# Low parts of 32 weight tiles made on GpSimd, with their loads and stores in its queue

## The chip, the cores and the metric

One core of a Trainium2 chip runs the kernel. The metric is the device time of one execution in microseconds (us); the median of three runs is compared. Engine names are those of the profile: PE is TensorE's matmul, PEld its weight load, ACT ScalarE, DVE VectorE, POOL GpSimd and SP SyncE; a q behind a name is the engine's instruction queue where it issues a DMA or waits.

## What is computed

One layer of a decoder block on a sequence of 1024 tokens with 1024 channels, in float32. The branch points are these:

```python
h = rms_norm(x, norm_gain) * (1.0 + scale) + shift      # scale, shift, gate from silu(c) @ w_ada + b_ada
q, k, v, z_a, u, z_b, m_a, m_b = split(h @ w_in)        # eight parts of 1024 columns
p_a = (stick_breaking_attention(q, k, v) * silu(z_a)) @ w_branch_a    # 16 heads of 64
p_b = (multiscale_causal_pool(u, pool_w, pool_scale) * silu(z_b)) @ w_branch_b
merged = sigmoid(m_a) * p_a + sigmoid(m_b) * p_b
out = rms_norm(x + gate * (merged @ w_out), final_gain)
```

## The kernel before

Every large product is made of three matmuls on TensorE. Each operand is split in two float32r parts: a high part, which is a copy of the operand, and a low part, the operand minus its high part. High by high, high by low and low by high are summed in PSUM. The weights come from HBM as float32 tiles of 128 x 1024, so each has to be split on the chip.

The stages follow one another on PE. First h is normed, turned and split, while the u projection of the first half of the tokens is begun. Then come the second half of u (to 128.7 us), the v projection (128.9 to 218 us), the eight z_b projections (tiles `wzb`, to 317.5 us), seven products of the pooling branch (names p1 to p7, to 395 us), then attention with the remaining 40 column tiles of w_in (k, q, z_a, m_a, m_b) projected between its steps (to 1032 us), and the end: w_branch_a, the merge, w_out and the last norm.

The 40 late column tiles are listed in `tiles`, in the order in which attention asks for them. For the first eight (`PLAIN`), `load_parts` splits the weight when it is needed, with the copy on ACT and the subtraction on POOL (or on DVE for one). For the other 32 the low part is made much earlier and put into an HBM tensor, `wl_d`; `load_parts` then reads the weight and the low part and only copies the high part again. Making it early is the work of `make_lo`, called once after each u tile (eight tiles), in the v loop by `LO_V` (ten), in the z_b loop by `LO_ZB` (four) and after the products by `LO_PB` (ten). A call takes a buffer tagged `lraw`, loads the weight into it, copies it to `lhi` (which has one buffer), subtracts `lhi` from `lraw` in place and stores the result. Within the v loop the last three steps are put off by one turn of the loop (`later=True`).

In the u and v stages these buffers lie in the pool `vp`, which is closed when v is done; its memory then goes to the pool `pb` of the z_b stage and the products. In `pb` the tag `lraw`, with three buffers, is also used by `gjunk` and by the gate weights `wg`: row j of w_gate is loaded, multiplied by silu(c), held in `sg`, and summed by DVE to one column of `gate`.

In the z_b stage PE writes halves of 24 matmuls into two PSUM banks in turn (tag `pj`). `silu` empties a bank: a sigmoid on ACT (L663) and a product on DVE (L664) that reads the bank; after L664 the bank is free. In the v stage L609 on ACT and L610 on DVE do the same.

The order of the instructions of each engine is drawn up ahead of time by a scheduler, which ranks them by their place in the program and by its own simulated times; where `order` or `keep_in_program_order` is used the program's order is kept, as in the first stage and in attention. The engines then run their queues strictly in that order. An instruction that has to wait, for a tile or for a buffer, holds everything behind it in its queue. Before the change SP's queue issues the loads and the stores of `make_lo`.

Of the kernel before, what the change touches and what calls it, by code (L numbers as in the profile page):

```python
# [9 lines left out]
F32 = mybir.dt.float32  # L10
F32R = mybir.dt.float32r
# [4 lines left out]
P = 128  # L16
D = 1024
# [23 lines left out]
LO_ZB = (0, 1, 0, 1, 0, 1, 0, 1)  # L41
LO_PB = (1, 2, 1, 2, 1, 2, 1)
# [15 lines left out]
def block_kernel(ctx, tc, a, out):  # L58
    nc = tc.nc
    v, act, gp = nc.vector, nc.scalar, nc.gpsimd  # L60

    def pool(name, **kw):
        return tc.tile_pool(name=name, bufs=1, reuse_waits="tile", **kw)
# [9 lines left out]
    def bank(tag, name):  # L73
        return psp.tile([P, 512], F32, tag=tag, bufs=BANKS[tag], name=name)
# [8 lines left out]
    wl_d = dram.tile([5 * KB, P, D], F32, name="wl_d")  # L83
# [37 lines left out]
    def copy_to(eng, dst, src):  # L121
        if eng is act:
            act.copy(dst, src)
        elif eng is gp:
            gp.tensor_scalar(dst, src, 1.0, 0.0, op0=ALU.mult, op1=ALU.add)
        else:
            v.tensor_copy(dst, src)
# [7 lines left out]
    tiles = []  # L135
# [6 lines left out]
    def make_lo(pl, n, bufs=3, later=False):  # L142

        rest = []
        for _ in range(n):
            i = next(early_lo)
            raw = pl.tile([P, D], F32, tag="lraw", bufs=bufs, name=f"l{i}_raw")
            hi = pl.tile([P, D], F32R, tag="lhi", bufs=1, name=f"l{i}_hi")
            nc.sync.dma_start(raw, a["w_in"][tiles[i]])

            def low(i=i, raw=raw, hi=hi):
                act.copy(hi, raw)  # L152
                v.tensor_sub(raw.bitcast(F32R), raw, hi.bitcast(F32))  # L153
                nc.sync.dma_start(wl_d[i], raw)

            if later:
                rest.append(low)
            else:
                low()
        return rest  # L160
# [27 lines left out]
    def project(ct, name, use, he, le):  # L188
        whl = load_w(a["w_in"][ct], name, he, le)
        for sh in range(2):  # L190
            ps = bank("pj", f"{name}_{sh}")
            mm3(ps, whl, (h_hi, h_lo), range(KB), hmov(sh))
            use(sh, ps)
# [18 lines left out]
    with pool("init") as init:  # L212
# [101 lines left out]
        wg, maps, halves = {}, {}, {}  # L314
# [66 lines left out]
        hi, lo_ = (0,), (1,)  # L381
# [172 lines left out]
    def load_u(j):  # L554
        u = dif.tile([P, S + 16], F32, tag="u", bufs=2, name=f"u{j}")
        v.memset(u[:, S:], 0.0)
        nc.sync.dma_start(u[:, :S], u_d[j])
        return u

    def make_d(j, u):  # L560
        win = WINDOWS[j // 2]
        cur, n, step = u, S + 16, 1
        while step < win:
            nxt = dif.tile([P, S + 16], F32, tag="win", bufs=2, name=f"win{j}_{step}")
            n -= step
            v.tensor_add(nxt[:, :n], cur[:, :n], cur[:, step:step + n])
            cur, step = nxt, 2 * step
        t0 = S - win + 1
        d = dif.tile([P, S], F32, tag="d", bufs=5, name=f"d{j}")
        v.scalar_tensor_tensor(d[:, :t0], cur[:, :t0], 1.0 / win, u[:, :t0], ALU.mult, ALU.subtract)  # L570
        tl = dif.tile([P, 16], F32, tag="tl", bufs=2, name=f"tl{j}")
        v.tensor_mul(tl[:, :win - 1], cur[:, t0:S], invn[:, 16 - win + 1:])
        v.tensor_sub(d[:, t0:], tl[:, :win - 1], u[:, t0:S])
        dhls[j] = d


    with pool("vp") as vp:
# [6 lines left out]
        for i in reversed(range(KB)):  # L584
            ps = bank("pj", f"u{i}_1")
            mm3(ps, whl[i], h, range(KB), hmov(1))
            use[i](1, ps)
            make_lo(vp, 1)
# [6 lines left out]
        for hf in range(2):  # L595
            if hf == 0:
                wv.append([load_wv(1, k2) for k2 in range(4)])
            for sb in range(8):
# [18 lines left out]
                if 8 * hf + sb in DIFFS:  # L617
                    j = DIFFS[8 * hf + sb]
# [8 lines left out]
    pb = pbs.enter_context(pool("pb"))  # L627
# [11 lines left out]
    def b_op(src, name):  # L639
        hl = pb.tile([P, 2, 2, 512], F32R, tag="bhl", bufs=3, name=name)  # L640
        act.copy(hl[:, 0], src)
        v.tensor_sub(hl[:, 1], src, hl[:, 0].bitcast(F32))
        return hl
# [7 lines left out]
    def a_op(src, name):  # L651
        hl = wts.tile([P, 2, 2, 512], F32R, tag="whl", bufs=2, name=name)
        act.copy(hl[:, 0], src)
        v.tensor_sub(hl[:, 1], src, hl[:, 0].bitcast(F32))
        return hl

    for j in range(KB):
        if j not in dhls:
            make_d(j, load_u(j))

        def silu(sh, ps):
            z = gb[:, j, sh * 512:sh * 512 + 512]
            act.activation(z, ps, AF.Sigmoid)  # L663
            v.tensor_mul(z, ps, z)  # L664
            v.scalar_tensor_tensor(z, dhls[j][:, sh * 512:sh * 512 + 512], psc_v[:, j:j + 1], z, ALU.mult, ALU.mult)

        project(CZB + j, f"wzb{j}", silu, act, v)
        if j < 4:
            v.tensor_sub(t1[:, j], gb[:, j, 512:], gb[:, j, :512])
        else:  # L670
            v.tensor_sub(t2[:, j - 4], gb[:, j, 512:], t1[:, j - 4])
            v.tensor_sub(gb[:, j - 4, 512:], gb[:, j, 512:], gb[:, j - 4, 512:])
        make_lo(pb, LO_ZB[j])
        if j == 0:
            nc.sync.dma_start(sg, a["c_row"].broadcast_to([P, D]))
            gjunk = pb.tile([P, D], F32, tag="lraw", bufs=3, name="gjunk")
            act.activation(gjunk, sg, AF.Sigmoid)
            v.tensor_mul(sg, sg, gjunk)
        wg = pb.tile([P, D], F32, tag="lraw", bufs=3, name=f"wg{j}")
        nc.sync.dma_start(wg, a["w_gate"][j])  # L680
        v.scalar_tensor_tensor(wg, wg, 1.0, sg, ALU.mult, ALU.mult, accum_out=gate[:, j:j + 1])
        del dhls[j]
# [50 lines left out]
    def out_b(j, n, t):  # L733
        nc.sync.dma_start(pb_d[j][:, 512 * n:512 * n + 512], t)

    def copied(tag, bufs, j, src):
        t = sums.tile([P, 512], F32, tag=tag, bufs=bufs, name=f"{tag}_{j}")
        act.copy(t, src)
        return t

    def added(t, src):
        v.tensor_add(t, src, t)
        return t

    for n, (name, a_of, b_of) in enumerate(products):
        c = {"p5": "b", "p3": "b", "p2": "c"}.get(name, "a")
        if c not in chain:
            chain[c] = [bank((tb if c == "b" else ta)[j], f"{name}_{j}") for j in range(4)]
        ps = chain[c]
        for q in range(2):  # L750
            wl_, ml_ = a_op(a_of(q), f"{name}a{q}"), b_op(b_of(q), f"{name}b{q}")
            for j in range(4):
                for e in range(2):
                    for i, (w, m) in enumerate(((0, 0), (0, 1), (1, 0))):
                        mm(
                            ps[j], wl_[:, w, e, j * P:(j + 1) * P], ml_[:, m, e],
                            start=name in ("p1", "p5", "p2") and (q, e, i) == (0, 0, 0), stop=(q, e, i) == (1, 1, 2),
                                skip_group_check=True,
                        )
        for j in range(4):  # L760
            if name == "p1":
                keep["s1", j] = copied("s1", 4, j, ps[j])
            elif name == "p6":
                keep["s2", j] = copied("s2", 4, j, ps[j])
            elif name == "p7":
                out_b(j + 4, 1, added(copied("s3", 2, j, ps[j]), chain["b"][j]))
            elif name == "p4":
                out_b(j + 4, 0, copied("s4", 2, j, ps[j]))
            elif name == "p3":
                out_b(j, 1, added(keep["s2", j], ps[j]))  # L770
            elif name == "p2":
                out_b(j, 0, added(keep["s1", j], ps[j]))
        make_lo(pb, LO_PB[n])
    pbs.close()


# [295 lines left out]
    with pool("fin") as fin:  # L1072
# [14 lines left out]
        for sh in range(2):  # L1087
            sl = slice(sh * 512, sh * 512 + 512)
            ms = []
            for j in range(KB):  # L1090
# [9 lines left out]
                n = 0  # L1100
# [12 lines left out]
            for i in range(4):  # L1113
# [8 lines left out]
                for c_, cl in enumerate(pieces):  # L1122
                    w_ = cl.stop - cl.start
                    ps = bank(("z", "tr")[c_ % 2], f"o{sb}_{c_}")[:, :w_]
                    n = 0
# [85 lines left out]
```

## Time and profile before

| | us |
|---|---|
| median of three runs (1213.62 to 1216.64) | 1214.39 |
| the profiled execution: its time | 1216.13 |
| the profiled execution: its span, first to last instruction | 1214.4 |
| mean granted TensorE clock, share of full speed | 0.996 |
| busy: PE, DVE, ACT, POOL | 1193.9, 796.0, 549.3, 168.8 |

A window row of the profile gives the stretch, its length, then busy time and number of instructions of PE, PEld, DVE, ACT and POOL, the granted TensorE clock, the busy share of the DMA engines and GB/s. A timeline row gives start, duration, engine, line, operation, out<-in with shapes, a count, and in brackets how long the engine had been idle and what ended that. A group row gives line, engine, operation, shapes and count, then total busy time and the mean in ns, then the idle time in front and its releasers. A row of a tile gives minimum, median and maximum duration in ns and the first and last start. A wait row reads: engine, line, what it waited for, total us, times, longest. Most matmuls are recorded under line 103 and many other helpers too, so the tile's name tells them apart.

### The profile page before, as it was taken

How to read it: one execution, taken by the hardware profiler on the slowest of the kernel's cores; microseconds unless marked ns; L12 is line 12 of the kernel's file. 1: busy time of each engine (PE TensorE's matmuls, PEld its weight loads, DVE VectorE, ACT ScalarE, POOL GpSimd, SP SyncE). 2: the span in 40 equal slices, each digit the busy share in tenths (PEclk: the TensorE clock that was granted, in tenths of full speed). 3: DMA queues.
4: the chain of work that ended last, by engine and by line, in shares of the span. 5: the costliest groups of instructions: out<-in, count | busy, mean ns of one | idle time of the engine just before them, and what ended most of it. 6: DMA issues, size and time to landing. Idle time of an engine off the chain costs nothing.

```text
span 1214.4 us, 16128 instructions
## 1 busy us (share of the span) xinstructions
PE 1193.9 (98%) x5698; PEld 995.1 (82%) x5698; DVE 796.0 (66%) x1088; ACT 549.3 (45%) x1020; POOL 168.8 (14%) x352
## 2 busy tenths in 40 slices
PE   8999999998999999999999999999999999999997
PEld 7888788876888888888888888888888888888876
DVE  5754473696765186777858678686777753785643
ACT  5564231332453255655655655555655653232211
POOL 1000000000000333222222221222221210000001
PEclk9999999998999999999999999999999999999999
DMA  9648895687725732343534325353353235984622
GB/s 355 253 172 320 317 364 211 215 261 210 268 86 187 229 81 72 116 129 99 165 114 141 106 88 165 109 157 106 107 140 100 96 124 195 335 276 162 208 73 83
DMA packets 85699, 212.39 MB, mean 175 GB/s; under 512 B 10609, under 2 KB 24049, under 8 KB 83442
## 3 DMA queue, kind: packets, MB, share of 16 engines
q1 hardware_dynamic: 77410, 196.47, 49.3%
q10 hardware_dynamic: 8208, 14.88, 3.3%
q8 instruction: 45, 0.74, 0.2%
q14 instruction: 36, 0.29, 0.1%
HBM read 144.20 MB, written 50.34 MB: 160 GB/s over the span
## 4 chain that ended last, share of the span: by engine, by line
PE 83%; DMA 7%; DVE 5%; issue 2%; ACT 1%; POOL 0%; SPq 0%; POOLq 0%; DVEq 0%; ACTq 0%
PE p L103 43%; PE o L103 6%; PE av L103 6%; PE z L103 6%; PE wt L103 5%; PE v L103 5%; PE pa L103 5%; DMA wl_d<-l_raw 3%; PE ua L103 3%; PE wzb L103 2%; DMA l_raw<-in_w_in 2%; PE u L103 2%; PE wm L103 1%; DVE l_raw L153 1%; DMA m<-sb_d 1%
## 5 line engine op out<-in xcount | busy, mean ns | idle before, releaser
L103 PE MATMUL p<-hT,w 128*128 128x512 f32 x1920 | 479.7, 391 | 0.0
L103 PEld LDWEIGHTS p<-hT,w 128*128 128x128 f32 x1920 | 355.3, 188 | 73.8 <-DVE klo L103 0.2
L933 DVE TENSOR_TENSOR_SCAN om<-om 128x512 f32<-128x512 f32 (+7 forms) x128 | 175.5, 1371 | 123.8 <-ACT om L926 69.0
L926 ACT ACTIVATE om<-z 128x512 f32<-128x512 f32 (+2 forms) x192 | 94.6, 493 | 156.0 <-PE z L103 133.2
L952 ACT CAST wt<-wt 128x512 fp32r<-128x512 f32 (+1 forms) x160 | 88.2, 551 | 48.1 <-PE wt L103 47.9
L953 DVE TENSOR_TENSOR wt<-wt,wt 128x512 fp32r<-128x512 f32 (+1 forms) x160 | 99.3, 620 | 16.1 <-ACT wt L952 15.5
L103 PE MATMUL av<-wt,vv 128*128 128x512 f32 x320 | 106.4, 414 | 0.0
L931 POOL TENSOR_SCALAR_AFFINE_SELECT om<-om 128x128 f32<-128x128 f32 x128 | 57.3, 448 | 345.6 <-ACT om L926 286.2
L103 PE MATMUL wzb<-hT,wzb 128*128 128x512 f32 x384 | 91.3, 399 | 8.4 <-DVE gb L664 8.4
L103 DVE TENSOR_TENSOR be<-be,om 128x511 f32<-128x511 f32 (+7 forms) x128 | 95.2, 749 | 1.1 <-POOL be L931 0.7
L103 PEld LDWEIGHTS wzb<-hT,wzb 128*128 128x128 f32 x384 | 73.7, 193 | 25.8 <-DVE gb L664 10.3
L927 ACT ACTIVATE be<-z 128x512 f32<-128x512 f32 (+2 forms) x192 | 94.0, 490 | 0.0
L103 PE MATMUL pa<-ga,wa 128*128 128x512 f32 x384 | 89.9, 390 | 1.0 <-DVE s L1105 1.0
L103 PE MATMUL o<-wo,mhl 128*128 128x512 f32 (+1 forms) x408 | 89.6, 377 | 0.0
L103 PE MATMUL wt<-ident,be 128*128 128x128 f32 x576 | 89.4, 273 | 0.0
L103 PE MATMUL v<-wv,hT 128*128 128x512 f32 x384 | 88.1, 390 | 1.2 <-DVE vo L610 1.2
L103 PEld LDWEIGHTS v<-wv,hT 128*128 128x128 f32 x384 | 71.9, 188 | 17.2 <-DVE vo L610 2.3
L103 PEld LDWEIGHTS pa<-ga,wa 128*128 128x128 f32 x384 | 71.9, 188 | 16.7 <-issue 1.3
L103 PEld LDWEIGHTS o<-wo,mhl 128*128 128x128 f32 x408 | 73.5, 188 | 14.1
L103 PEld LDWEIGHTS wt<-ident,be 128*128 128x128 f32 x576 | 70.2, 141 | 11.6
L152 ACT CAST l_hi<-l_raw 128x1024 fp32r<-128x1024 f32 x32 | 33.7, 1052 | 80.5 <-DMA l_raw<-in_w_in 74.4
L153 DVE TENSOR_TENSOR l_raw<-l_raw,l_hi 128x1024 fp32r<-128x1024 f32 x32 | 39.2, 1224 | 44.1 <-ACT l_hi L152 43.9
(175 smaller groups left out, 1476.5 us busy)
## 6 DMA issues: line engine op xcount, KB each, us to landing
w_raw<-in_w_in SPq DMA_DIRECT2D x40, 512.0 KB, 4.5
l_raw<-in_w_in SPq DMA_DIRECT2D x32, 512.0 KB, 5.3
wl_d<-l_raw SPq DMA_DIRECT2D x32, 512.0 KB, 5.9
w<-wl_d SPq DMA_DIRECT2D x32, 512.0 KB, 3.8
v_d<-vo SPq DMA_DIRECT2D x16, 512.0 KB, 4.8
vv<-v_d SPq DMA_DIRECT2D x8, 1024.0 KB, 5.4
wa_raw<-in_w_branch_a SPq DMA_DIRECT2D x16, 512.0 KB, 4.7
wa<-in_w_mod SPq DMA_DIRECT2D x7, 1024.0 KB, 7.3
```

The lines of the kernel that those rows point to most:

```text
L103: ins = op(*args, **kw)
L152: act.copy(hi, raw)
L153: v.tensor_sub(raw.bitcast(F32R), raw, hi.bitcast(F32))
L926: act.activation(om[:, b0:b0 + n], zp[:, :n], AF.Sigmoid, scale=-0.125)
L927: act.activation(be[:, b0:b0 + n], zp[:, :n], AF.Sigmoid, scale=0.125)
L931: gp.affine_select(out=tl[:, :P], in_=tl[:, :P], pattern=[[1, P]], compare_op=ALU.is_gt, fill=fill, base=0, channel_multiplier=-1)
L933: v.tensor_tensor_scan(om[:, :W], om[:, :W], om[:, :W], 1.0, ALU.mult, ALU.min)
L952: act.copy(wt[:, 0, :off], pt[:, :off])
L953: v.tensor_sub(wt[:, 1, :off], pt[:, :off], wt[:, 0, :off].bitcast(F32))
```

## The change

`make_lo` moves to POOL whole: the load is issued by POOL, the high part is copied there (as a multiplication by one and an addition of zero, `copy_to`), the subtraction runs there, and POOL issues the store. In `pb` the weight buffers become two, and `gjunk` and the gate rows get a tag of their own with one buffer.

```diff
@@ make_lo
             raw = pl.tile([P, D], F32, tag="lraw", bufs=bufs, name=f"l{i}_raw")
             hi = pl.tile([P, D], F32R, tag="lhi", bufs=1, name=f"l{i}_hi")
-            nc.sync.dma_start(raw, a["w_in"][tiles[i]])
+            gp.dma_start(raw, a["w_in"][tiles[i]])
 
             def low(i=i, raw=raw, hi=hi):
-                act.copy(hi, raw)
-                v.tensor_sub(raw.bitcast(F32R), raw, hi.bitcast(F32))
-                nc.sync.dma_start(wl_d[i], raw)
+                copy_to(gp, hi, raw)
+                gp.tensor_sub(raw.bitcast(F32R), raw, hi.bitcast(F32))
+                gp.dma_start(wl_d[i], raw)
@@ the z_b loop
-        make_lo(pb, LO_ZB[j])
+        make_lo(pb, LO_ZB[j], 2)
         if j == 0:
             nc.sync.dma_start(sg, a["c_row"].broadcast_to([P, D]))
-            gjunk = pb.tile([P, D], F32, tag="lraw", bufs=3, name="gjunk")
+            gjunk = pb.tile([P, D], F32, tag="wg", bufs=1, name="gjunk")
             act.activation(gjunk, sg, AF.Sigmoid)
             v.tensor_mul(sg, sg, gjunk)
-        wg = pb.tile([P, D], F32, tag="lraw", bufs=3, name=f"wg{j}")
+        wg = pb.tile([P, D], F32, tag="wg", bufs=1, name=f"wg{j}")
@@ after each product
-        make_lo(pb, LO_PB[n])
+        make_lo(pb, LO_PB[n], 2)
```

## The prediction

> **What bounds the kernel now.** I read the first lines of the page, then the stages by window, then PE's own waits, and last the queues of ACT and DVE around the stall.
>
> ```profile
> PE 1193.9 (98%) x5698; PEld 995.1 (82%) x5698; DVE 796.0 (66%) x1088; ACT 549.3 (45%) x1020; POOL 168.8 (14%) x352
> ...
> L152 ACT CAST l_hi<-l_raw 128x1024 fp32r<-128x1024 f32 x32 | 33.7, 1052 | 80.5 <-DMA l_raw<-in_w_in 74.4
> L153 DVE TENSOR_TENSOR l_raw<-l_raw,l_hi 128x1024 fp32r<-128x1024 f32 x32 | 39.2, 1224 | 44.1 <-ACT l_hi L152 43.9
> ```
>
> TensorE is busy for 98% of the span, so the 72.9 us that leave ACT and DVE (33.7 + 39.2) are worth only what PE waits for them. PE's busy time, in the windows that the low parts occupy, is the third column here, with PEclk further right:
>
> ```profile
> 96.00:157.00 61.00, 60.00 (x263) 49.20 (x263) 27.21 (x32) 22.10 (x28) 0.00 (x0) 1.00 0.88 315
> 230.00:280.00 50.00, 45.99 (x201) 37.13 (x199) 48.74 (x66) 18.91 (x23) 0.00 (x0) 1.00 0.82 242
> 280.00:317.00 37.00, 32.64 (x131) 26.20 (x130) 23.01 (x28) 11.69 (x14) 0.00 (x0) 0.91 0.78 266
> 317.00:395.00 78.00, 78.00 (x342) 63.99 (x341) 50.20 (x50) 34.69 (x43) 2.42 (x1) 1.00 0.47 162
> ```
>
> Waiting shows between 230 and 317 us, the stage of the eight z_b projections (wzb), and one microsecond in the v stage; from 317 us on PE has no hole. POOL's column is empty in the whole stretch up to 317. PE's waits by releaser and the wzb stage in order of time:
>
> ```profile
> PE wzb L103 <- DVE gb L664: 8.4, 4, 4.4
> PE v L103 <- DVE vo L610: 1.2, 2, 1.0
> ...
> 217.99 38.24 PE L103 MATMUL wzb<-hT,wzb 128*128 128x512 f32 x168
> 257.73 5.74 PE L103 MATMUL wzb<-hT,wzb 128*128 128x512 f32 x24 [1.50 <-DVE gb L664]
> 264.79 11.17 PE L103 MATMUL wzb<-hT,wzb 128*128 128x512 f32 x48 [1.32 <-DVE gb L664]
> 277.14 16.79 PE L103 MATMUL wzb<-hT,wzb 128*128 128x512 f32 x72 [1.19 <-DVE gb L664]
> 298.29 19.35 PE L103 MATMUL wzb<-hT,wzb 128*128 128x512 f32 x72 [4.36 <-DVE gb L664]
> ```
>
> There are two kinds of hole. Three of 1.2 to 1.5 us (4.0 in sum) fall where DVE is full: 48.74 of 50 us. The fourth, 4.36 us, falls where DVE is idle for over a third of the time, and there the order of the queues does it:
>
> ```profile
> 295.33 1.04 ACT L152 CAST l_hi<-l_raw 128x1024 fp32r<-128x1024 f32 x1 [4.74 <-DMA l_raw<-in_w_in]
> 296.29 0.59 ACT L663 ACTIVATE gb<-wzb 128x512 f32<-128x512 f32 x1
> ...
> 296.41 1.23 DVE L153 TENSOR_TENSOR l_raw<-l_raw,l_hi 128x1024 fp32r<-128x1024 f32 x1 [3.89 <-ACT l_hi L152]
> 297.55 0.68 DVE L664 TENSOR_TENSOR gb<-wzb,gb 128x512 f32<-128x512 f32 x1
> ```
>
> ACT stood 4.74 us waiting for a weight to land, with the sigmoid that empties PE's bank behind it; DVE stood 3.89 us the same way. After that hole PE is also slow: 72 matmuls took 19.35 us, where the first stretch (38.24 us for 168) makes 16.39 of them. That is 2.96 us, at a granted clock of 0.91 over the window.
>
> **The change part by part, against the profiled span of 1214.4 us.**
>
> **Casts off ACT, subtractions off DVE.** The 32 low parts no longer stand in either queue. What that frees in each window:
>
> ```profile
> 230.00:280.00 50.00, 8.57 (x7) 7.38 (x7) 1.00 0.82 242
> 280.00:317.00 37.00, 8.58 (x7) 7.35 (x7) 0.91 0.78 266
> ```
>
> No landing of a low-part weight can stop ACT or DVE any more, so the 4.36 us hole should go, and with it the 2.96 us of slow clock. The v wait of 1.2 us had the same sort of queue before it (DVE's low parts and window sums ahead of L610); I count it as gone. Sum so far: 4.36 + 2.96 + 1.2 = 8.5 us.
>
> For the three holes under a full DVE, 8.57 us of 48.74 leave it: 40.2 us in 50. Against that POOL now reads SBUF beside DVE, and that costs something:
>
> ```profile
> 571.31 1.65 POOL L931 TENSOR_SCALAR_AFFINE_SELECT be<-be 128x128 f32<-128x128 f32 x1 [0.20 <-ACT be L927]
> ...
> 571.66 1.21 DVE L933 TENSOR_TENSOR_SCAN om<-om 128x512 f32<-128x512 f32 x1
> ...
> 589.58 0.74 POOL L982 TENSOR_TENSOR tp<-tp,za 128x256 f32<-128x256 f32 x1 [4.95 <-DVE tp L979]
> ...
> 590.13 1.13 DVE L103 TENSOR_TENSOR be<-be,om 128x895 f32<-128x895 f32 x1
> 573.37 1.07 DVE L103 TENSOR_TENSOR be<-be,om 128x895 f32<-128x895 f32 x1
> ...
> L931 POOL TENSOR_SCALAR_AFFINE_SELECT be<-be x128: 283/292/1647, 421.5 to 997.5; 128x128 f32<-128x128 f32 x128
> ```
>
> A select that mostly takes 0.29 us took 1.65 and ended 0.09 us after a DVE scan did: POOL was held up. The other way round, a DVE product that began 0.19 us before a POOL instruction ended took 1.13 us instead of 1.07. The Trainium skill, SBUF — State Buffer, section "Who interferes with whom", says that a VectorE instruction with two SBUF inputs and a GpSimd instruction that reads SBUF exclude each other, the later one blocking fully. The trace agrees for POOL (1.65 against 0.29 us) and has no long POOL read ahead of such a DVE instruction; by the rule the sum is the second rival's, by the rows the one that follows.
>
> DVE's loss in the 50 us is thus between nothing and all of POOL's reading time there (22.7 us, below). I take about half, 11 us: DVE is back at 51 us and the three holes stay as they are, worth 0. Ends: 4.0 us gained if DVE loses nothing, 8.9 lost if it loses all (40.2 + 22.7 - 50 = 12.9 us of holes in place of 4.0).
>
> **Loads and stores in POOL's queue, and what a tile costs there.** Nothing shows a copy of this size on POOL or a DMA issued by it. Nearest rows, for compute and transfers (the last two are median times to landing):
>
> ```profile
> L118 POOL TENSOR_TENSOR w<-w_raw,w 128x1024 fp32r<-128x1024 f32 x7 | 16.8, 2399 | 351.4 <-ACT w L123 346.3 <-DMA w_raw<-in_w_in 5.1
> L785 POOL MEMSET kl<- 64x1024 f32 x4 | 3.8, 949 | 0.2
> ...
> L149 SPq DMA_DIRECT2D l_raw<-in_w_in x32: 327/332/577, 69.4 to 308.8; - x32
> L152 ACT CAST l_hi<-l_raw x32: 1044/1052/1057, 91.2 to 312.4; 128x1024 fp32r<-128x1024 f32 x32
> ...
> 220.49 0.94 SPq L675 DMA_DIRECT2D sg<-in_c_row  x1
> ...
> 221.96 0.43 SPq L149 DMA_DIRECT2D l_raw<-in_w_in  x1
> ...
> l_raw<-in_w_in SPq DMA_DIRECT2D x32, 512.0 KB, 5.3
> wl_d<-l_raw SPq DMA_DIRECT2D x32, 512.0 KB, 5.9
> ```
>
> The subtraction is the very shape of L118: 2.4 us. The copy has one input: at least the memset's 0.95, at most the two-input 2.4; I take 1.1, near the memset, since it also streams one tensor. An issue is at least SP's 0.33 us and at most another whole-tile POOL instruction, 2.4; I take 0.33, the row of the same transfer. A tile is then 0.33 + 1.1 + 2.4 + 0.33 = 4.2 us of POOL, between 4.0 and 9.6. The Trainium skill, DMA: Bandwidth & Descriptors, section "Latency and other measured facts", gives a software-generated DMA a first-byte latency of about 1 us; put in for both issues as an estimate that makes 5.5 us a tile, which no run here shows and which leaves the sum as it is.
>
> Each load waits for the store that last used its buffer, and behind it in POOL's queue stand the next copy, subtraction and store. One turn of a buffer is 0.33 + 5.3 + 1.1 + 2.4 + 0.33 + 5.9 = 15.4 us. With three buffers, as in the u and v stages, that is a tile every 5.1 us: 18 tiles from 91 us (the first cast of before, 91.2) take 92 us and end at 183, plus a landing, before PE leaves the v stage at 218. With two, as in the pool of wzb and the products, it is 7.7 us: 14 tiles from 222 us (the first load of that pool, 221.96) end at 330. In the v stage DVE is busy for 27.21 of 61 us, so collisions there find room. POOL's next own work and the first reader of a low part are later:
>
> ```profile
> 390.23 2.42 POOL L118 TENSOR_TENSOR w<-w_raw,w 128x1024 fp32r<-128x1024 f32 x1 [322.87 <-ACT w L123]
> ...
> L168 SPq DMA_DIRECT2D w<-wl_d x32: 319/320/542, 495.4 to 1009.7; - x32
> ```
>
> So 60 us of slack cover POOL, and the attention's selects queue behind nothing: 0. In the 50 us window 6.5 tiles run, reading for 3.5 us each: the 22.7 us above. If the cover goes, the price is the third rival's.
>
> **SP's queue** loses 64 issues and their waits on stores. Past that lie v's stores, u, wv, wzb and gate loads and the branch weights; none of them releases PE in the waits above, so 0, and with nothing to pay should that be wrong.
>
> **Buffers.** Two weight buffers instead of three are in the 7.7 us. The gate rows (wg) get one buffer of their own:
>
> ```profile
> wg<-in_w_gate SPq DMA_DIRECT2D x8, 512.0 KB, 4.4
> ...
> L681 DVE SCALAR_TENSOR_TENSOR wg<-wg,sg x8: 1217/1219/1225, 228.3 to 262.9; 128x1024 f32<-128x1024 f32 x8
> ```
>
> One turn is 0.33 + 4.4 + 1.22 = 6.0 us against 4.9 now (34.6 us for seven steps); eight need 48 us of a stage of 99. Spread out that costs 0; if DVE's order has them back to back, DVE stands up to 7 x 4.4 = 31 us there. I take 0, since a projection lasts 11 us and asks for one row.
>
> **Sum.** 8.5 us off, 1205.9 us span. The profiled execution took 1216.13 us, 1.74 above the median of the three runs, so the gain goes on the median: 1214.39 - 8.5 = 1205.9, say 1206.
>
> **The rivals.**
>
> *Everything comes back.* If DVE loses nothing to POOL, the three holes go too: 8.5 + 4.0 = 12.5 us, 1202. For it: 40.2 us in 50 leaves room. Against it: POOL's selects show that the two do collide.
>
> *POOL and DVE trade places.* All POOL reads of the window fall on DVE, or the single gate buffer makes DVE stand: 8.9 us of new holes against 8.5 saved, 1215 (with half of that, 1210). For it: the 1.65 us select and the full DVE of 230 to 280 us. Against: the DVE row lost 0.06 us.
>
> *POOL is late (slower).* One mechanism: POOL's cost per tile. It decides at (218 - 91)/18 = 7.05 us: above it the low parts outlast the v stage, whose memory the next pool takes. The pool's first load, sg, and the DVE product that needs it stand in front of the next L664:
>
> ```profile
> 227.07 1.23 DVE L678 TENSOR_TENSOR sg<-sg,gjunk 128x1024 f32<-128x1024 f32 x1 [1.34 <-ACT gjunk L677]
> ```
>
> At 8 us a tile the last store lands at 91 + 144 + 5.9 = 241, the sg load comes 20 us after its 220.5 of now, and PE, which can run one bank of 24 matmuls (5.4 us) ahead, stalls about 15: 1214.4 + 15 - 8.5 = 1221. At the 9.6 us end it is some 45 us, 1251. For it: POOL's waits of up to 1.4 us for DVE per instruction and the unknown issue. Against: taken costs of 4.2, or 5.1 by buffers.
>
> **How the numbers follow.** Likeliest 0.42, with 1203 to 1210 as its own range; everything back 0.20; trading places 0.23; POOL late 0.15. A difference under 0.3% (3.6 us) is about what a measurement of this kernel cannot tell from none. Faster: the first two and a little of the third, 0.64; same: most of the third, 0.20; slower: POOL late and the third's tail, 0.16. The range runs from 1201, just under everything back, to 1220, where the late case begins.
>
> **What would show it.** Right: no ACT or DVE wait with l_raw in it; the 4.36 us hole gone and the clock at 1.0 from 280 to 317 us; POOL's l rows over by about 330 us; PE waits on L664 of about 4 us. Wrong: POOL subtractions well over 2.4 us with issues over 1 us, low parts still running at 218, sg late, DVE products longer or idle before a two-input instruction, or DVE waiting for wg to land. The scheduler also draws up the order of all unpinned queues anew; a new order that puts another wait ahead of L664 or L610 would spoil the sum in either direction, and I price it at 0. A PE wait past 390 us with a POOL releaser would break the claim that slack covers POOL.

## The result and the profile after

| | before | after |
|---|---|---|
| median of four runs, us | 1214.14 | 1233.66 |
| ratio, 95% interval | | 1.0166, 1.0131 to 1.0200 |
| span of the profiled execution, us | 1214.4 | 1230.6 |
| mean granted TensorE clock | 0.996 | 0.992 |

The changed kernel is slower by 1.7%. The change costs 19.5 us by the medians and 16.2 us by the spans of the two profiles. The busy totals of the changed kernel:

```profile
PE 1198.8 (97%) x5698; PEld 997.3 (81%) x5698; DVE 805.6 (65%) x1056; ACT 518.4 (42%) x988; POOL 328.5 (27%) x480
```

DVE was to lose 39.2 us of subtractions and come to 796.0 - 39.2 = 756.8. It stands at 805.6, 48.8 us higher. A busy total counts the time in which two instructions overlap once; summed one by one, the DVE instructions that stayed take 856.8 us where they took 811.6, so they are stretched by 45.2 us. The rest is overlap with the subtractions that left; the writing-only run below ends 4.0 us above 756.8 with no stretch at all. POOL took on 328.5 - 168.8 = 159.7 us, 5.0 us a tile.

The same windows as before (the fourth field is DVE's time in the order PE, PEld, DVE, ACT, POOL; the granted clock stands behind them):

```profile
96.00:157.00 61.00, 57.94 (x255) 47.33 (x254) 27.22 (x24) 10.24 (x15) 47.30 (x41) 1.00 0.88 295
157.00:218.00 61.00, 53.81 (x223) 43.10 (x222) 37.38 (x34) 9.38 (x13) 42.23 (x32) 0.94 0.82 291
230.00:280.00 50.00, 43.46 (x176) 35.00 (x175) 39.66 (x41) 9.36 (x13) 27.48 (x23) 0.93 0.68 224
280.00:317.00 37.00, 32.31 (x134) 25.90 (x133) 32.74 (x36) 7.68 (x10) 22.47 (x18) 0.95 0.67 208
317.00:395.00 78.00, 78.00 (x343) 64.08 (x342) 50.41 (x49) 33.40 (x43) 7.48 (x6) 1.00 0.51 159
```

In the first window DVE runs 24 instructions where it ran 32, in the same 27.2 us. In the second PE loses 7 us, in the v stage, where before it hardly waited. None of these windows has a full DVE: 37.4 of 61 us, 39.7 of 50, 32.7 of 37. From 317 us on PE is whole again. PE's waits by releaser:

```profile
PE wzb L103 <- DVE gb L664: 11.2, 4, 3.4
PE v L103 <- DVE vo L610: 10.1, 4, 4.7
```

That is 21.3 us against 9.6 before, 11.7 more. The rest is PE's slower pace behind the holes, at granted clocks of 0.93 to 0.95. At the undisturbed rate of before (38.24 us for 168 matmuls, 227.6 ns each) the 223, 176 and 134 matmuls of the three windows with holes would take 121.3 us; they took 129.6, so 8.3 us went to the slower pace. The same sum over 230 to 317 us of before gives 3.1. Together 11.7 + 5.2 = 16.9 us, and the spans differ by 16.2.

One hole of the v stage, POOL, DVE, ACT and PE in order of time:

```profile
153.05 2.40 POOL L153 TENSOR_TENSOR l_raw<-l_raw,l_hi 128x1024 fp32r<-128x1024 f32 x1
153.30 3.25 DVE L570 SCALAR_TENSOR_TENSOR d<-win,u 128x1021 f32<-128x1021 f32 x1
...
158.68 1.26 POOL L125 TENSOR_SCALAR l_hi<-l_raw 128x1024 fp32r<-128x1024 f32 x1 [1.82 <-DMA l_raw<-in_w_in]
...
159.07 1.94 DVE L570 SCALAR_TENSOR_TENSOR d<-win,u 128x1021 f32<-128x1021 f32 x1
159.20 0.58 ACT L609 CAST vo<-v 128x512 fp32r<-128x512 f32 x1 [7.47 <-PE v L103]
160.02 3.18 POOL L153 TENSOR_TENSOR l_raw<-l_raw,l_hi 128x1024 fp32r<-128x1024 f32 x1
160.93 2.29 DVE L572 TENSOR_TENSOR tl<-win,invn 128x3 f32<-128x3 f32 x1
163.15 0.68 DVE L610 TENSOR_TENSOR vo<-v,vo 128x512 fp32r<-128x512 f32 x1
...
163.88 6.38 PE L103 MATMUL v<-wv,hT 128*128 128x512 f32 x16 [4.72 <-DVE vo L610]
...
166.16 3.23 POOL L153 TENSOR_TENSOR l_raw<-l_raw,l_hi 128x1024 fp32r<-128x1024 f32 x1
167.09 0.68 DVE L610 TENSOR_TENSOR vo<-v,vo 128x512 fp32r<-128x512 f32 x1
```

Alone, the product and the three columns take much less; these rows are from the kernel before:

```profile
160.00 1.22 DVE L570 SCALAR_TENSOR_TENSOR d<-win,u 128x1021 f32<-128x1021 f32 x1
161.13 0.15 DVE L572 TENSOR_TENSOR tl<-win,invn 128x3 f32<-128x3 f32 x1
```

Read each end against the next start. POOL's subtraction ends at 155.45; DVE's product L570, begun at 153.30, ends 1.10 us after that: it stood for 2.0 us and then ran. At 159.07 the next L570 meets a copy that ends at 159.94, and ends 1.07 us later. POOL's subtraction of 160.02 in turn stands until that L570 ends at 161.01, and ends 2.19 us later, at 163.20. Behind it DVE holds three columns of L572 for 2.29 us, until the same moment. Each instruction here waits for the whole of the one that came first, and the two engines take turns. Three held instructions, 2.0 + 0.7 + 2.1 = 4.9 us, stand in DVE's order ahead of L610, which empties PE's bank; ACT had its half ready at 159.78. PE waits 4.72 us.

The groups of DVE over 72 to 334 us that suffer, after and then before (count, busy time, mean ns of one):

```profile
L665 DVE SCALAR_TENSOR_TENSOR gb<-d,vecs,gb 128x512 f32<-128x512 f32 x15 | 17.6, 1170 | 0.3
L118 DVE TENSOR_TENSOR wv<-wv_raw,wv 128x1024 fp32r<-128x1024 f32 x8 | 17.2, 2179 | 7.4 <-ACT wv L123 7.4
...
L153 POOL TENSOR_TENSOR l_raw<-l_raw,l_hi 128x1024 fp32r<-128x1024 f32 x32 | 86.3, 2698 | 2.4
L125 POOL TENSOR_SCALAR l_hi<-l_raw 128x1024 fp32r<-128x1024 f32 x32 | 38.3, 1197 | 65.4 <-DMA l_raw<-in_w_in 65.1
```

```profile
L665 DVE SCALAR_TENSOR_TENSOR gb<-d,vecs,gb 128x512 f32<-128x512 f32 x16 | 11.9, 750 | 0.2
L118 DVE TENSOR_TENSOR wv<-wv_raw,wv 128x1024 fp32r<-128x1024 f32 x8 | 9.7, 1222 | 8.9 <-ACT wv L123 8.9
```

POOL is in a reading instruction for 86.3 + 38.3 = 124.6 us; DVE's 45.2 us are 36% of that. The DVE instructions that empty a bank, with one operand in PSUM, keep their time: the L610 of 167.09 takes its 0.68 us beside the subtraction that runs until 169.39.

### The profile page after: what moved, and what is told of

It is laid out like the page before. It is cut to its first block, busy times and chain, and to the rows that moved or that the text cites. A ratio compares the mean times of both kernels' runs of the same rounds, so it can differ in the third digit from the quotient of the medians.

```text
span 1230.6 us, 16069 instructions
## 1 busy us (share of the span) xinstructions
PE 1198.8 (97%) x5698; PEld 997.3 (81%) x5698; DVE 805.6 (65%) x1056; ACT 518.4 (42%) x988; POOL 328.5 (27%) x480
## 4 chain that ended last, share of the span: by engine, by line
PE 80%; DMA 7%; DVE 6%; issue 4%; SPq 1%; ACT 0%; POOL 0%; POOLq 0%; ACTq 0%; DVEq 0%
PE p L103 38%; PE pa L103 7%; PE o L103 6%; PE z L103 5%; PE av L103 5%; PE wt L103 5%; PE u L103 4%; PE v L103 3%; PE ua L103 3%; DMA u<-u_d 2%; PE wzb L103 2%; DMA wg<-in_w_gate 2%; DVE win L566 1%; DVE wg L681 1%; DMA wa<-in_w_mod 1%
## 5 line engine op out<-in xcount | busy, mean ns | idle before, releaser
L103 PE MATMUL wzb<-hT,wzb 128*128 128x512 f32 x384 | 93.2, 405 | 11.2 <-DVE gb L664 11.2
L103 PE MATMUL v<-wv,hT 128*128 128x512 f32 x384 | 91.3, 399 | 10.2 <-DVE vo L610 10.1
L103 PEld LDWEIGHTS wzb<-hT,wzb 128*128 128x128 f32 x384 | 75.2, 197 | 29.1 <-DVE gb L664 12.9
L153 POOL TENSOR_TENSOR l_raw<-l_raw,l_hi 128x1024 fp32r<-128x1024 f32 x32 | 86.3, 2698 | 2.4
L103 PE MATMUL z<-kl,q 128*128 128x512 f32 (+2 forms) x192 | 65.5, 341 | 0.0
```

Of the source, the lines that this page charges most:

```text
L103: ins = op(*args, **kw)
L153: gp.tensor_sub(raw.bitcast(F32R), raw, hi.bitcast(F32))
```

## Experiments

Ratios are to the kernel before, with 95% intervals; the line numbers of some variants are one to three higher than the changed kernel's.

**The parts of the change one by one.** The first two put copy and subtraction back on ACT and DVE; one of them keeps the transfers on POOL.

```diff
 e1: the changed kernel with
-            gp.dma_start(raw, a["w_in"][tiles[i]])
+            nc.sync.dma_start(raw, a["w_in"][tiles[i]])
-                copy_to(gp, hi, raw)
-                gp.tensor_sub(raw.bitcast(F32R), raw, hi.bitcast(F32))
-                gp.dma_start(wl_d[i], raw)
+                act.copy(hi, raw)
+                v.tensor_sub(raw.bitcast(F32R), raw, hi.bitcast(F32))
+                nc.sync.dma_start(wl_d[i], raw)
 e2: only copy and subtraction so; both dma_start stay on gp
```

> Casts, subtractions, loads and stores of the low parts go back to ACT, DVE and SP; only two weight buffers instead of three and the gate rows' single buffer remain of the change. Port theory (GpSimd's reads of SBUF hold up DVE's instructions with two SBUF inputs): nothing is left of the loss, 1208 to 1218 us, DVE durations as before. Buffer theory (DVE stands for the single gate buffer, 7.6 us of waits on wg in the changed kernel): at least 5 us slower than before, 1219 us or more, with waits of DVE on wg.

Measured: 1217.21 us, ratio 1.0026 (1.0016 to 1.0036). This is inside the range expected if POOL's reads are the cause. The buffers alone, with the order that the scheduler draws for them, cost 2.7 us. PE's waits in front of wzb are 3.6 us more than before, and those in the v stage are gone:

```profile
PE wzb L103 <- DVE gb L664: 12.0, 5, 5.6
```

> The changed kernel with the cast back on ACT and the subtraction back on DVE; GpSimd only issues the loads and stores. Port theory: GpSimd reads no SBUF here, so no DVE instruction is stretched and the time is that of buffers only or less, 1205 to 1218 us. Theory that the software-issued transfers in GpSimd's queue cost the time: 1225 us or more.

Measured: 1221.85 us, ratio 1.0062 (1.0047 to 1.0077), between the two ranges: above the one expected if POOL's reads are the cause and below the one expected if the transfers are. DVE is not stretched (796.2 us busy), but POOL's own queue now holds the transfers:

```profile
POOL wl_d L154 <- DVE l_raw L153: 97.2, 24, 33.2
...
POOL l_raw L149 <- DMA wl_d<-l_raw: 80.4, 23, 9.0
```

A store that waits for DVE's subtraction stands ahead of the next load, so loads go out late and ACT and DVE meet weights that have not landed: PE's waits for L664 are 9.5 us in front of wzb and 3.2 in front of the products. This part of the cost is one of this variant; in the changed kernel POOL makes the low part itself.

```diff
 e3: the changed kernel with only the transfers back on SP
-            gp.dma_start(raw, a["w_in"][tiles[i]])
+            nc.sync.dma_start(raw, a["w_in"][tiles[i]])
-                gp.dma_start(wl_d[i], raw)
+                nc.sync.dma_start(wl_d[i], raw)
```

> The changed kernel with the loads and stores back in SP's queue; GpSimd only casts and subtracts. Port theory: as slow as the changed kernel, 1227 to 1240 us, DVE busy about 49 us more than its instructions take alone. Theory of the software-issued transfers: 1205 to 1218 us.

Measured: 1238.75 us, ratio 1.0202 (1.0186 to 1.0217). The compute carries the loss; issuing the transfers on POOL as well costs nothing on top (the intervals of this variant and the changed kernel overlap, so whether it gains is open). DVE is stretched as in the changed kernel:

```profile
L665 DVE SCALAR_TENSOR_TENSOR gb<-d,vecs,gb 128x512 f32<-128x512 f32 x15 | 17.8, 1190 | 0.3
```

**POOL's reading taken away.** About the same time on POOL (3.4 us a tile), the same transfers and buffers, but instructions that only write; the low parts are then left out of the result:

```diff
-                copy_to(gp, hi, raw)
-                gp.tensor_sub(raw.bitcast(F32R), raw, hi.bitcast(F32))
+                gp.memset(raw, 0.0)
+                gp.memset(hi.bitcast(F32), 0.0)
+                gp.memset(raw, 0.0)
+                gp.memset(raw[:, :512], 0.0)
```

> The changed kernel with GpSimd's cast and subtraction replaced by memsets of the same two tiles, of about the same total length (3.4 us a tile), so the low parts are left out of the results. GpSimd then writes SBUF and reads none of it. Port theory, reads: DVE's instructions take what they take alone (L665 0.75 us instead of 1.17), PE's waits on L610 and L664 shrink from 21 us to under 8, 1200 to 1212 us. Any theory by which GpSimd's length, its queue or the buffers cost the time: 1225 us or more.

Measured: 1204.52 us, ratio 0.9926 (0.9904 to 0.9948), with DVE busy 760.8 us; one by one its instructions take 811.2 us, as before without the subtractions (811.6). Two windows and the group of L665 (here L667):

```profile
157.00:218.00 61.00, 58.99 (x261) 48.54 (x260) 22.55 (x31) 9.99 (x14) 34.88 (x49) 1.00 0.90 326
230.00:280.00 50.00, 50.00 (x221) 41.09 (x220) 44.50 (x62) 12.99 (x17) 25.76 (x36) 1.00 0.82 270
```

```profile
L667 DVE SCALAR_TENSOR_TENSOR gb<-d,vecs,gb 128x512 f32<-128x512 f32 x16 | 12.0, 748 | 0.4
```

PE has no hole at all from 230 to 280 us, at the full clock, and L665 is back at 748 ns. Of DVE's 1056 instructions all but 25 run in the same sequence as in the changed kernel, so the order is nearly the same. So the change without POOL's reads is worth 10.0 us by the medians (9.0 by the ratio), and POOL's reads take back 1233.66 - 1204.52 = 29.1.

**Where the hold comes from.** If each DVE instruction waits out one POOL instruction, shorter POOL instructions hold it for less.

```diff
+                for b in range(0, D, 256):
+                    copy_to(gp, hi[:, b:b + 256], raw[:, b:b + 256])
+                for b in range(0, D, 256):
+                    gp.tensor_sub(raw[:, b:b + 256].bitcast(F32R), raw[:, b:b + 256], hi[:, b:b + 256].bitcast(F32))
-                copy_to(gp, hi, raw)
-                gp.tensor_sub(raw.bitcast(F32R), raw, hi.bitcast(F32))
```

> The changed kernel with GpSimd's cast and subtraction cut into four instructions of 256 columns each, the same arithmetic. Hold by instruction (a DVE instruction waits until the GpSimd instruction in progress is over): one wait is at most about 0.7 us instead of 2.4, DVE's L665 comes to under 1.0 us on the mean instead of 1.17, and the time to 1210 to 1228 us. Shared bandwidth (both engines slowed in proportion to what they read): the same bytes, so 1228 to 1240 us as in the changed kernel.

Measured: 1223.80 us, ratio 1.0068 (1.0052 to 1.0085): 9.9 us better than whole instructions. The tile's rows (minimum, median and maximum ns) and the group from 96 to 317 us:

```profile
L125 POOL TENSOR_SCALAR l_hi<-l_raw x128: 394/408/1477, 91.5 to 375.4; 128x256 fp32r<-128x256 f32 x128
L155 POOL TENSOR_TENSOR l_raw<-l_raw,l_hi x128: 714/733/1815, 93.0 to 377.8; 128x256 fp32r<-128x256 f32 x128
```

```profile
L667 DVE SCALAR_TENSOR_TENSOR gb<-d,vecs,gb 128x512 f32<-128x512 f32 x14 | 14.1, 1007 | 0.2
```

The mean of L665 comes to 1007 ns (1275 over the same stretch of the changed kernel), a little over the bound of the hold theory; the time is in its range. DVE's stretch falls only from 45.2 to 38.6 us (busy 798.8): it is held more often, for less each time. PE's waits for L610 and L664 fall more, from 21.3 to 14.7 us, which fits that the length of one hold ahead of them counts for more than the sum; no run here varies the one without the other.

Which of POOL's two instructions holds DVE:

```diff
 e6: the changed kernel with
-                gp.tensor_sub(raw.bitcast(F32R), raw, hi.bitcast(F32))
+                v.tensor_sub(raw.bitcast(F32R), raw, hi.bitcast(F32))
 e7: the changed kernel with
-                copy_to(gp, hi, raw)
+                act.copy(hi, raw)
```

> The changed kernel with the subtraction back on DVE; GpSimd keeps the cast (one input, 1.06 us) and the transfers. If any GpSimd read holds DVE: some 30% of the changed kernel's GpSimd reading time (1.06 of 3.5 us a tile) is left, DVE's two-input instructions are stretched by 10 to 20 us in sum, and with the 39 us of subtractions back on DVE the time is 1224 to 1235 us. If only a GpSimd instruction with two inputs holds DVE: no stretch, as with transfers alone, 1217 to 1224 us.

> The changed kernel with the cast back on ACT; GpSimd keeps the subtraction (two inputs, 2.4 us) and the transfers. If any GpSimd read holds DVE: two thirds of the stretch stay, 28 to 40 us of the 49, and the time is 1224 to 1236 us, ACT standing for landings again. If the cast were what holds DVE (its reads and writes alone): no stretch, under 1215 us.

Measured: the copy alone on POOL 1225.11 us, 1.0086 (1.0071 to 1.0101); the subtraction alone 1232.00, 1.0136 (1.0114 to 1.0159). L665 over 72 to 334 us, in the first and in the second:

```profile
L665 DVE SCALAR_TENSOR_TENSOR gb<-d,vecs,gb 128x512 f32<-128x512 f32 x16 | 13.4, 843 | 0.2
```

```profile
L665 DVE SCALAR_TENSOR_TENSOR gb<-d,vecs,gb 128x512 f32<-128x512 f32 x16 | 17.4, 1087 | 0.3
```

Both hold, and both times are in the range expected if any read on POOL does. The copy reads one operand only and still does. Summed one by one, DVE is stretched by 10.7 us in the first and 31.9 in the second, together close to the 45.2 of the changed kernel. The times do not add up so (10.5 and 17.4 us over the kernel before, against 19.5); each variant also keeps one step that waits across engines in somebody's queue.

**Another way to the same gain.** The holes of the kernel before came from low parts in ACT's and DVE's order ahead of L663 and L664. They can be kept off that place without POOL. Here, in the kernel before, the sigmoids, their products and the ten low parts of `LO_PB` keep the program's order (`pin` wraps load, copy and subtraction in `keep_in_program_order`):

```diff
-            act.activation(z, ps, AF.Sigmoid)
-            v.tensor_mul(z, ps, z)
+            tc.keep_in_program_order(act.activation(z, ps, AF.Sigmoid))
+            tc.keep_in_program_order(v.tensor_mul(z, ps, z))
...
-        nc.sync.dma_start(wg, a["w_gate"][j])
+        tc.keep_in_program_order(nc.sync.dma_start(wg, a["w_gate"][j]))
...
-        make_lo(pb, LO_PB[n])
+        make_lo(pb, LO_PB[n], pin=True)
```

> The kernel before, with the ten low parts of the products' stage kept behind the last z_b projection in the order of SP, ACT and DVE (in before they ran in the middle of the z_b stage). If, as the prediction had it, PE's waits in the z_b stage come from low parts in ACT's and DVE's queues, 8.4 us of waits there fall to under 3 and the time to 1203 to 1210 us, faster than both kernels. If DVE is simply too full in that stage for other reasons, the waits stay at 6 us or more and the time at 1211 to 1218; if the products' stage has no room for ten low parts, PE waits there by 4 us or more and it is slower than before.

Measured: 1215.89 us, ratio 1.0012 (1.0003 to 1.0022). The wzb holes are gone, 8.4 us down to 1.0, with DVE still busy for 46.1 of the 50 us from 230 on. The loss came back at the end of the products:

```profile
PE p L103 <- DVE klo L103: 6.6, 2, 4.2
PE p L103 <- ACT p3a L654: 2.0, 1, 2.0
```

The last low part was subtracted at 394.5 us, in the way of attention's first steps. So the ten were moved forward:

```diff
-LO_PB = (1, 2, 1, 2, 1, 2, 1)
+LO_PB = (2, 2, 2, 2, 2, 0, 0)      # e9
+LO_PB = (3, 3, 2, 2, 0, 0, 0)      # e10
```

> The kernel before, with its ten low parts of the product stage kept behind the last z_b projection as in the run with late low parts, but spread (2, 2, 2, 2, 2, 0, 0) over the seven products instead of (1, 2, 1, 2, 1, 2, 1). If what ate the gain there was only that the last low parts stood in DVE's queue ahead of attention's first instructions, the waits of PE for klo and p3a (8.6 us) go, the z_b stage stays near 1 us of waits with the clock at 1.0, the last low part is over before 375 us, and the time is 1203 to 1208 us, ratio 0.990 to 0.995. If a low part costs PE about the same wherever it stands in DVE's and ACT's queues, the waits come back inside the products and the time stays at 1212 to 1217, ratio 0.998 to 1.002.

> As the run beside it with (3, 3, 2, 2, 0, 0, 0): the low parts end earlier still, by about 350 us, but three buffers allow one per 4.7 us (load 5.3, cast 1.05, subtraction 1.22, store 5.9, two issues, over three), so more of them wait for a landing in ACT's queue early in the products. If only the end of the stage matters: 1203 to 1208, ratio 0.990 to 0.995, equal to its neighbour within 2 us. If landings held in ACT's and DVE's queues hurt wherever PE needs a bank emptied: slower than its neighbour by 2 to 8 us.

Measured: 1212.04 us, 0.9979 (0.9966 to 0.9991), and 1210.45 us, 0.9975 (0.9958 to 0.9991). Half of the hoped gain or less: the last subtraction came at 385.9 us, not before 375, and at 384.0, not at 350, and one wait for klo stayed (4.8 and 3.7 us). The first variant's window shows what may have slowed them, by its last two numbers, the DMA engines' busy share and GB/s; the same window of the kernel before follows:

```profile
340.00:400.00 60.00, 57.62 (x251) 46.40 (x249) 34.00 (x35) 27.64 (x33) 11.00 (x7) 1.00 0.90 308
```

```profile
340.00:400.00 60.00, 60.00 (x264) 49.25 (x263) 31.02 (x32) 25.24 (x31) 6.59 (x4) 1.00 0.46 164
```

The low parts' loads and stores had been spread over the z_b stage; pushed into the products they fill the DMA engines. So some go back to the z_b stage, but with the copy put off by one projection, as in the v loop, so that the weight has landed when ACT comes to it:

```diff
-        make_lo(pb, LO_ZB[j])
+        for f in todo:
+            f()
+        todo = make_lo(pb, LO_ZB[j], later=True, pin=True)
...
-LO_ZB = (0, 1, 0, 1, 0, 1, 0, 1)
-LO_PB = (1, 2, 1, 2, 1, 2, 1)
+LO_ZB = (0, 1, 0, 1, 1, 1, 1, 1); LO_PB = (2, 2, 2, 2, 0, 0, 0)      # e11
+LO_ZB = (0, 1, 0, 1, 1, 1, 2, 2); LO_PB = (2, 2, 2, 0, 0, 0, 0)      # e12
```

> The kernel before with the low parts of the z_b stage put off by one projection (load in one turn, cast and subtraction after the next pair of sigmoids, so the weight has landed when ACT reaches the cast), six of them there and eight after the products as (2, 2, 2, 2, 0, 0, 0). If waits for a landing in ACT's and DVE's order are what PE paid for in the kernel before, and the rest that was lost in the two runs before this was a full transfer queue from 340 to 400 us (busy share 0.79 to 1.0), then the z_b stage stays under 1.5 us of waits, the wait for klo falls from 3.7 to under 2, and the time is 1203 to 1208 us, ratio 0.990 to 0.995. If DVE's fullness alone makes the z_b holes, the two more low parts bring 2.5 us of them back and the time is 1209 to 1213.

> As its neighbour with eight low parts in the z_b stage, as (0, 1, 0, 1, 1, 1, 2, 2), and six after the products, as (2, 2, 2, 0, 0, 0, 0). By landings and transfers: no wait for klo above 1 us, 1202 to 1207 us, ratio 0.990 to 0.994, the best of these. By DVE's fullness: 1210 to 1215.

Measured: e11 1217.93 us, 1.0027 (1.0017 to 1.0037), outside both expectations; e12 1207.51 us, 0.9938 (0.9924 to 0.9952), half a microsecond above the range expected by landings, with the ratio inside it and no wait for klo. In both PE has no wait for wzb. e11 lost it in the products, where PE waits 6.5, 3.4 and 1.4 us for ACT. The longest is one landing, in ACT's queue and then PE's; its rows and its window:

```profile
338.68 1.04 ACT L153 CAST l_hi<-l_raw 128x1024 fp32r<-128x1024 f32 x1 [13.52 <-DMA l_raw<-in_w_in]
...
343.65 8.06 PE L103 MATMUL p<-p6b,p6a 128*128 128x512 f32 x24 [6.53 <-ACT p6a L654]
```

```profile
325.00:340.00 15.00, 12.12 (x47) 9.48 (x45) 6.50 (x7) 1.21 (x2) 0.00 (x0) 0.89 1.03 144
```

The DMA engines are busy throughout and move only 144 GB/s; a store of `gate` went out just ahead of the two loads. Whether that store filled them was not tried. e12 has nearly the same window (0.94, 163 GB/s), but no landing of a low-part weight that ACT waits for there, and ACT's longest such wait in the products is 2.0 us. A full transfer queue is thus not enough to explain the runs before: from 340 to 400 us e12's DMA engines are busy for 0.87 at 300 GB/s, about as in e9, and PE does not wait for klo. Why these spreads differ as they do stays open. e12 beats the kernel before by 0.6% and the changed one by 26 us, with copy and subtraction where they had been.

## Why the prediction was wrong, point by point

**The step that failed** is DVE's loss to POOL's reads: its size outside the one window that was priced, and what it does to PE. The prediction took "about half, 11 us" of it in the window from 230 to 280 us, let the holes there "stay as they are, worth 0", put the v stage at nothing ("collisions there find room") and gave the window from 280 to 317 us no price. Summed one by one, DVE's instructions lost 10.5 us in that window, 9.7 from 280 to 317 us, and 11.2 and 12.9 us in the two windows of the v stage, 45.2 us in all. PE waited 21.3 us for L610 and L664 where it had waited 9.6. That loss is the whole sign of the result: with POOL writing only, the time was 1204.5, within the forecast's own range of 1203 to 1210.

So the 11 us were near the mark, by luck: they were half of a bound, chosen by a row that could not show more. A product that began 0.19 us before a POOL instruction ended can lose at most 0.19 us, so 0.06 bounded nothing; the trace of before had no whole-tile read on POOL ahead of a DVE instruction of that kind, and of the rows quoted only the 1.65 us select was one of a full collision. The rule of the Trainium skill, SBUF — State Buffer, section "Who interferes with whom", which the prediction gave, says that the later of the two blocks fully; the traces agree (3.25 us for a 1.22 us product, 3.18 for a 2.40 us subtraction, and no stretch when POOL only wrote).

What turned the result is the measure. Idle time of DVE was taken as cover, by averages over a window. A held instruction does not move to an idle stretch; it stands in order ahead of L610 or L664, and PE has one bank in hand. Holds of 2.0, 0.7 and 2.1 us used it up at 163 us, while DVE was idle for 24 of the 61 us of that window.

**The three holes** were said to stay, under a full DVE. PE does stand before wzb, for 11.2 us, but DVE is not full there (39.7 of 50 us); the writing-only run, with nearly the same order, has 0.3 us of such waits, so they are new holes with the cause above. That a full DVE made the old ones (48.7 of 50 us) is not shown: they are gone with 44.5 us of 50 in the writing-only run, but also with 46.1 in e8, where ten low parts are kept behind the projections and nothing is taken off DVE.

**The 4.36 us hole and the v wait** went in the writing variant, which fits the reason given; in the changed kernel the waits in the v stage grew to 10.1 us, and the clock from 280 to 317 us was 0.95 and not 1.0. The writing variant gained 10.0 us where the prediction had 8.5 for these and 12.5 with the three holes; it kept a v wait of 2.0.

**POOL's cost per tile** was close: predicted 4.2 us, with copy 1.1, subtraction 2.4 and issues of 0.33. The rows:

```profile
L149 POOL DMA_DIRECT2D l_raw<-in_w_in x32: 532/604/767, 67.2 to 322.8; - x32
L125 POOL TENSOR_SCALAR l_hi<-l_raw x32: 1042/1061/1959, 91.0 to 329.1; 128x1024 fp32r<-128x1024 f32 x32
L153 POOL TENSOR_TENSOR l_raw<-l_raw,l_hi x32: 2370/2408/3373, 92.1 to 330.2; 128x1024 fp32r<-128x1024 f32 x32
L154 POOL DMA_DIRECT2D wl_d<-l_raw x32: 533/542/615, 95.7 to 333.6; - x32
```

The medians make 4.6 us; an issue is 0.54 to 0.60, not 0.33, and DVE's holds bring the mean to 5.0. The last store is issued at 333.6 us (330 predicted), and that agreement is luck: the first load of the z_b pool's tiles went out at 205.4 us and not at 222, and the 14 tiles took 9.2 us each and not 7.7. There a load was issued only when the subtraction of the tile before had ended (one at 238.07 us, behind a subtraction until 238.12), so the two buffers hardly overlapped. The 18 tiles before them were done at 202.7 us, 6.2 us each where 5.1 were predicted; the rival of a late POOL, at 7.05 us a tile, did not come about.

**The buffers** were priced at 0 and cost 2.7 us alone. The single gate buffer does what the prediction named for it, DVE standing for a row ahead of L664; in the changed kernel that is 7.6 us in four waits, one of them here, in front of a product that POOL then holds (ACT, DVE and PE):

```profile
253.76 0.59 ACT L663 ACTIVATE gb<-wzb 128x512 f32<-128x512 f32 x1
...
254.68 2.58 DVE L681 SCALAR_TENSOR_TENSOR wg<-wg,sg 128x1024 f32<-128x1024 f32 x1 [1.90 <-DMA wg<-in_w_gate]
...
259.47 0.68 DVE L664 TENSOR_TENSOR gb<-wzb,gb 128x512 f32<-128x512 f32 x1
...
260.21 7.33 PE L103 MATMUL wzb<-hT,wzb 128*128 128x512 f32 x24 [3.27 <-DVE gb L664]
```

Since the writing variant kept these buffers, with 6.7 us of such DVE waits, and had 0.3 us of wzb waits, they decide nothing without the holds.

**The rival "trade places"** had the mechanism and was sized at 8.9 us of holes, in one window. Measured against no holds, POOL's reads cost 29.1 us over two stages.

## What to carry to other kernels

Before work goes to GpSimd beside a busy VectorE, list the VectorE instructions with two SBUF operands that stand ahead of the one that frees TensorE's bank: in this kernel each could be held for a whole GpSimd read, 2.4 us, however short it was and however idle VectorE was on average. Where that is the case, write-only work may go there, or GpSimd's instructions may be cut smaller, which gave back 9.9 of the 29.1 us here. If the trouble is an instruction that waits for a landing ahead of a critical one, put it off until the data are there and keep it in that order: in one spread that gave 0.6% here without moving any work to another engine, and in the other it lost 0.3%, so the spread has to be tried.

## What the runs showed of the hardware that was not expected

The hold did not depend on the size of what was held. One column per partition waited out a whole subtraction:

```profile
141.04 2.45 POOL L153 TENSOR_TENSOR l_raw<-l_raw,l_hi 128x1024 fp32r<-128x1024 f32 x1
141.15 2.35 DVE L573 TENSOR_TENSOR d<-tl,u 128x1 f32<-128x1 f32 x1
```

That instruction took 0.16 us on average before. A GpSimd copy with a single operand holds VectorE as well (L665 843 ns against 750), a fill does not (748). A 512 KB transfer issued by GpSimd takes 0.54 to 0.60 us of its queue, by the medians.
